# Modulations of the first gated network: from weighted row sums turned by TensorE to one multiply-and-sum per transposed weight tile

## The chip, the core and the metric

The kernel runs on one core of a Trainium2 chip. Its work is shared by TensorE (matrix products, PE in the profile, PEld for its weight loads), VectorE (DVE), ScalarE (ACT), GpSimd (POOL) and SyncE (SP), which here issues nearly all transfers; 16 DMA engines carry them. Each engine has a queue of its own and works it off in order. The metric is the device time of one execution in microseconds, as a median of several runs.

## The reference

A decoder trunk of two layers over 512 tokens of 1024 channels. The first layer mixes tokens with a state-space layer (S5), the second with forgetting attention; behind each stands a gated network with a convolution of width 3. So there are four sub-layers, numbered 0 to 3: S5, first gated network, attention, second gated network. Each is modulated by one conditioning vector `c` of 1024 numbers:

```python
def adaln_params(c, w, b):
    mod = jax.nn.silu(c) @ w + b
    shift, scale, gate = jnp.split(mod, 3, axis=-1)

def modulate(x, g, shift, scale):
    return rmsnorm(x, g) * (1.0 + scale) + shift

hn = modulate(h, norm_g[i, 1], shift, scale)
f = conv_ffn(hn, ffn_w_up[i], ffn_conv_w[i], ffn_conv_b[i], ffn_w_down[i])
h = (h + gate * f).astype(x.dtype)
```

The weights `w` of one modulation are 1024 x 3072 in float32, 12 MB for each sub-layer. The three thirds of its result are the shift (third 0), the scale (third 1) and the gate (third 2). What the change touches is how `silu(c) @ w + b` is computed for some of these thirds.

## The kernel before, in words

Channels lie on the 128 partitions and tokens along the free dimension; 1024 channels are 8 such tiles (`KT`). Large products are made in three parts from a high and a low part of each factor (L301 in the helper `mms`): ScalarE rounds a weight tile to its high part (L284), VectorE subtracts to get the low part (L285), TensorE multiplies three times.

A modulation is wanted in columns: `par[i]` holds for sub-layer i 24 columns of 128 partitions (shift in 0 to 7, scale in 8 to 15, gate in 16 to 23), since channels lie on partitions. `ga[i]` is (1 + scale) times the norm's weight, 8 columns. `sc` is silu(c) as 128 x 8, made by ScalarE at the very start (L102).

There are two ways in which the kernel makes them:

- `ada_pe`, in the S5 stage, for sub-layer 0 and for shift and scale of sub-layer 1: weight tiles go through TensorE against `sc` (L217), and the row that comes out is turned into columns by `ada_columns`.
- `ada_units`, in the first gated network, for the gate of sub-layer 1 and all thirds of sub-layers 2 and 3: seven thirds in five groups ([2] of 1, [0, 1] and [2] of 2, [0, 1] and [2] of 3). For each third, eight tiles of 128 x 1024 (128 of the 1024 inputs, all 1024 outputs of the third) are loaded into two buffers (L240). VectorE multiplies each by the column of `sc` for these inputs and adds it to an accumulator of 128 x 1024 (L243 for the first tile, L245 for the other seven). TensorE then sums the accumulator over partitions by products with ones (L251, four to a third in the profile), ScalarE copies the rows (L255). At the end of a group, `ada_columns` turns the rows into columns on TensorE: the bias comes in by a product with the identity (L160), the rows by products with a selector (L165), and VectorE and ScalarE write `ga` (L170) and `par` (L173).

The work of `ada_units` is cut into steps, one for each weight tile. `build` puts the five groups on the list `bg`, and the gated network takes one step (`tick`) after each of its products: 22 up products, 8 down products, 22 up, and 6 of the last down products (the last two belong to the tail). The 56 tiles fit these 58 ticks. The first of them is taken after the first up product.

The compiler's scheduler sets the order on each engine from when it expects operands to be ready, except in the first part of S5, where `manual_schedule` keeps the order of the program on TensorE, ScalarE, VectorE and SP. In the gated network one rule is written by hand: the first VectorE instruction of each third is put behind the last low part that the norm has made (`issue_after(self.last_lo.ins)`).

The network's head (its first three up products) is worked by halves of the tokens: while TensorE multiplies the first half, the statistics of the second half's norm are taken by TensorE (L385), VectorE makes the inverse root from them (L396 to L406), TensorE spreads it to rows (L415), VectorE multiplies by `ga` (L435), ScalarE makes the high part (L438) and VectorE the low part (L439).

At the start of the kernel SP issues, in this order: the parameters with `c`, x in four pieces of 512 KB, the rest of the constants, then the weights of the modulation of sub-layer 0 for `ada_pe` (L188), S5's first weights and constants.

The attention has a VectorE instruction that adds, takes the minimum along the free dimension and writes both (L1445), followed in the profile by a read of the accumulator.

Of the kernel before, what the change touches and what calls it, by code (L numbers as in the profile page):

```python
# [8 lines left out]
F32 = mybir.dt.float32  # L9
F32R = mybir.dt.float32r  # L10
I32 = mybir.dt.int32
AF = mybir.ActivationFunctionType
ALU = mybir.AluOpType
# [4 lines left out]
P = 128  # L18
D = 1024
KT = D // P  # L20
S = 512
# [22 lines left out]
TAIL_OFF = {"w_hi": 80, "w_lo": 112}, {"w_hi": 96, "w_lo": 0}  # L44

GROUPS = (11, 11)
QGROUPS = (6, 5, 6, 5)
TAIL = 4
FIRST = (("c", (KT,)), ("s5_prm", (3, G // 2)), ("s5_eye", (64,)))
# [12 lines left out]
class Trunk:  # L62
# [138 lines left out]
    def ada_pe(self, i, thirds, late=False):  # L201
# [9 lines left out]
        for step in steps:  # L211
# [15 lines left out]
                self.ada_columns(i, 8 * thirds[0], 8 * thirds[-1] + 8, rows)  # L227
            yield True

    def ada_units(self, i, thirds):  # L230

        nc = self.nc
        thirds = list(thirds)
        rows = self.bgpool.tile([P, S], F32, name="ada_rows", bufs=1)
        n = 0
        for t in thirds:
            acc = self.bgpool.tile([P, D], F32, name="ada_acc", bufs=1)
            for k in range(KT):
                w = self.bgpool.tile([P, D], F32, name="ada_raw", bufs=2)
                nc.sync.dma_start(w, self.io["ada_w"][i, k * P:(k + 1) * P, t * D:(t + 1) * D])  # L240
                if k == 0:
                    with self.tc.issue_after(self.last_lo.ins):
                        nc.vector.tensor_scalar(acc, w, self.sc[:, 0:1], None, op0=ALU.mult)  # L243
                else:
                    nc.vector.scalar_tensor_tensor(  # L245
                        acc, w, self.sc[:, k:k + 1], acc, op0=ALU.mult, op1=ALU.add
                    )
                if k == KT - 1:
                    ps = self.aux.tile([P, S], F32, name="aux")
                    for q in range(2):  # L250
                        nc.tensor.matmul(  # L251
                            ps[32 * q:32 * q + 32, :], self.ones[:, :32], acc[:, q * S:(q + 1) * S],
                            start=True, stop=True, tile_position=(0, 32 * q), skip_group_check=True,
                        )
                    nc.scalar.activation(rows[32 * n:32 * n + 64], ps[:64], AF.Copy)  # L255
                    n += 2
                    if t == thirds[-1]:
                        self.ada_columns(i, 8 * thirds[0], 8 * thirds[-1] + 8, rows[:32 * n])
                yield True


    def finish_norm(self, n=NORM_AFTER):

# [323 lines left out]
    def ffn(self, i, l, x, nxt, ticks=0, plain=None):  # L587

        nc, tc = self.nc, self.tc
        with tc.tile_pool(name=f"ffn{l}", bufs=1, reuse_waits="tile") as pool:  # L590
            self.bgpool = pool
            groups = QGROUPS if plain else GROUPS
            first = [sum(groups[:q]) for q in range(len(groups) + 1)]
            keep, g = {}, {}

            def gate_room(q):
                tag = f"{q % 2}" if plain else ""
                g[q] = [pool.tile([P, groups[q], S], F32R, name=n, tag=n + tag) for n in ("ghi", "glo")]

            if plain:  # L600
                self.gap(pool, 32, "g_gap")
                gate_room(0)
                b = [pool.tile([P, KT // 2, S], F32, name=f"x{j}", tag=n) for j, n in enumerate(("ghi1", "glo1"))]
            conv = self.wide(pool, "conv_wb", {}, F32, 0 if plain else 8, 0, [P, 4, FT])
            nc.sync.dma_start(conv, self.io["conv"][l])
            cw, cb = conv[:, :3], conv[:, 3]

            def gated(m, ps, cols):
                f = m // 2
                if m % 2 == 0:  # L610
                    t = pool.tile([P, S], F32, name="conv", bufs=2 if plain else 3)
                    nc.scalar.activation(t, ps, AF.Identity, bias=cb[:, f:f + 1], scale=cw[:, 2, f:f + 1])
                    for d in (1, 2):
                        nc.vector.scalar_tensor_tensor(  # L614
                            t[:, d:], ps[:, :S - d], cw[:, 2 - d, f:f + 1], t[:, d:], op0=ALU.mult, op1=ALU.add
                        )
                    nc.scalar.activation(t, t, AF.Silu)  # L617
                    keep[f] = t
                    return
                t = keep.pop(f)  # L620
                nc.vector.tensor_tensor(t, t, ps, ALU.mult)
                q = sum(f >= n for n in first[1:])
                j = f - first[q]
                if q not in g:
                    gate_room(q)
                hi, lo = g[q]
                self.put_parts(hi[:, j, :], lo[:, j, :], t)

            after, y = nxt
            def up(fs, **k):  # L630
                self.odd = bool(plain)
                self.product(self.io["w_up"][l], range(2 * fs[0], 2 * fs[-1] + 2), KT, x, gated, ticks=ticks, **k)
                self.odd = False

            last = len(groups) - 1
            down = lambda q, ms, **k: self.product(
                self.io["w_down"][l][:, :, first[q]:first[q + 1], :], ms, groups[q], g[q],
                self.add_residual(i, q == last), after=after, ticks=ticks, **k
            )
            todo = []  # L640
            for q, n in enumerate(groups):
                fs = range(first[q], first[q + 1])
                if not plain:
                    up(fs, head=0 if q else 3)
                    if q < last:
                        down(q, range(KT))
                    continue
                for j, f in enumerate(fs):
                    if f == 0:
                        up([0, 1], head=3, apart=True)  # L650
                        todo.append(self.forms_x(pool, x, b))
                    elif f in plain:
                        if f > 1:
                            up([f], apart=True)
                        for _ in range(4):
                            if todo and next(todo[0], True):
                                todo.pop()
                    else:
                        while todo:
                            if next(todo[0], True):  # L660
                                todo.pop()
                        self.quarters(pool, l, f, x, gated)
                    if q:
                        down(q - 1, range(j * KT // n, (j + 1) * KT // n))
            down(last, range(KT), tail=TAIL if plain else 2, tail_pool=(pool, 4, TAIL_OFF[l]))
        return y
# [121 lines left out]
class S5(Trunk):  # L788
# [291 lines left out]
    def s5(self, i, nxt):  # L1080
        nc, tc = self.nc, self.tc
# [4 lines left out]
        with ExitStack() as stack:  # L1086
# [3 lines left out]
            with ExitStack() as start:  # L1090
                tp = spool("s5t", start)
                self.load_first(tp)
                w = {}
# [9 lines left out]
                with tc.manual_schedule(engines={ENG.PE, ENG.Activation, ENG.DVE, ENG.SP}):  # L1103
                    self.load_x(self.act)
                    self.load_rest()
                    self.s5_planes(keep)
                    ps = self.mm.tile([P, S], F32, name="mmp")
                    for k in range(KT):
# [3 lines left out]
                    rows = self.tmp.tile([P, S], F32, name="nm_t")  # L1112
# [19 lines left out]
                    ps = self.mm.tile([P, S], F32, name="mmp")  # L1132
# [29 lines left out]
            pool = self.s5r = spool("s5r", stack)  # L1162
# [86 lines left out]
            next(ada[1])  # L1249
        self.load_x(self.ctx.enter_context(tc.tile_pool(name="resid", bufs=1, reuse_waits="tile")))  # L1250
        with tc.tile_pool(name="s5b", bufs=1, reuse_waits="tile") as pool:
            self.bgpool = pool
            self.gap(pool, 32, "z_gap")
            zhi = pool.tile([P, KT, S], F32R, name="zhi")
            zlo = pool.tile([P, KT, S], F32R, name="zlo")

            def glu(m, ps, cols):
                t = self.tmp.tile([P, S], F32, name="nm_t")
                nc.scalar.activation(t, ps, AF.Sigmoid)  # L1259
                nc.vector.tensor_tensor(tok(t), tok(t), self.s5_read_y(pool, m), ALU.mult)  # L1260
                self.put_parts(zhi[:, m], zlo[:, m], t)

            for m in range(HEAD):
                glu(m, gps[m], slice(0, S))
            self.product(self.io["s5_w_glu"], range(HEAD, KT), KT, (yhi, ylo), glu)
            after, y = nxt
            self.product(self.io["s5_w_out"], range(KT), KT, (zhi, zlo), self.add_residual(i), tail=2, after=after)
# [245 lines left out]
def lay_out(inp):  # L1513

    f = {n: np.asarray(v) for n, v in inp.items()}
    o = {}
# [8 lines left out]
    o["c"] = cols(f["c"][0], KT)  # L1525
    o["ident"] = np.eye(P, dtype=np.float32)
    o["ada_w"] = f["ada_w"].reshape(4, D, 3 * D)
    o["ada_b"] = cols(f["ada_b"].reshape(4, 3 * D), 24)
    o["norm_g"] = cols(f["norm_g"].reshape(4, D), KT)
    o["final_g"] = cols(f["final_g"], KT)  # L1530
# [22 lines left out]
    w = f["fox_w_in"][0]  # L1553
# [38 lines left out]
```

## Time and profile before

| | |
|---|---|
| median of 3 runs (lowest to highest) | 1244.78 us (1244.68 to 1244.86) |
| the profiled execution's own time | 1247.16 us |
| its span, first to last instruction | 1245.4 us |
| mean granted TensorE clock | 0.993 |
| first gated network, about | 262 to 640 us |
| weight tiles of `ada_units` loaded (first to last issue) | 56 of 512 KB (270.2 to 577.6 us) |
| data moved over the span | 183.24 MB |

How to read it: times are microseconds from the span's start. Engine busy times overlap, so they don't add up to the span. The chain of work that ended last is followed back from the last instruction, at each step to what released it or to the instruction before it on its engine; what doesn't lie on it could be shorter without the end moving at once. A group's row gives line, engine, operation, tile written and tiles read, shapes and count, then busy time and the mean of one in ns, then the idle time ahead of it and what ended that. In a row of the waits stand the engine that waited, what it waited for, the total, the number of times and the longest. A row of the transfers gives the count, the size of one and the median time from issue to landing.

### The profile page before, as it was taken

What the parts mean: (1) busy time and instruction counts of PE and PEld (TensorE: products, weight loads), DVE (VectorE), ACT (ScalarE), POOL (GpSimd) and SP (SyncE); (2) the same over time, 40 slices, a digit from 0 to 9 for tenths busy, and PEclk for the clock granted to TensorE, in tenths of its full rate; (3) what the DMA queues carried; (4) which work ended last, traced back from release to release, by engine and by line L of the source; (5) the groups of instructions that cost most, each with busy time, mean ns of one, the idle gap of its engine ahead of it and who ended that gap; (6) DMA issues with size and microseconds to landing.
All of it is one profiled execution on the core that took longest, in us unless ns stands there. A gap on an engine that the chain in (4) does not pass through costs nothing.

```text
span 1245.4 us, 19609 instructions
## 1 busy us (share of the span) xinstructions
PE 1221.6 (98%) x7584; PEld 1023.6 (82%) x7584; DVE 896.0 (72%) x1610; ACT 564.9 (45%) x1043; POOL 57.1 (5%) x109
## 2 busy tenths in 40 slices
PE   7999999999999999999999999999989999999997
PEld 2566677898778887788799888888989999999987
DVE  7978886569756547566457467665799978888865
ACT  3543455335333223333434366654456555555543
POOL 0000000000000000000000143331000000000000
PEclk9999999999999999999999999999999999999999
DMA  9768667336745646455423344240313332333331
GB/s 353 249 226 261 197 180 255 102 110 193 252 133 176 197 157 219 139 182 165 142 68 102 126 137 134 94 141 15 124 47 113 108 117 89 112 107 106 102 85 69
DMA packets 73068, 183.24 MB, mean 147 GB/s; under 512 B 23079, under 2 KB 25471, under 8 KB 71951
## 3 DMA queue, kind: packets, MB, share of 16 engines
q1 hardware_dynamic: 72687, 181.46, 45.2%
q8 instruction: 60, 0.98, 0.3%
q10 hardware_dynamic: 288, 0.52, 0.1%
q14 instruction: 33, 0.27, 0.1%
HBM read 175.04 MB, written 6.92 MB: 146 GB/s over the span
## 4 chain that ended last, share of the span: by engine, by line
PE 93%; DVE 2%; DMA 2%; issue 1%; ACT 1%; SPq 0%; DVEq 0%; ACTq 0%
PE mmp L301 57%; PE mmp L556 10%; PE mmp L1171 4%; PE aux L556 4%; PE mmp L1337 3%; PE aux L976 2%; PE aux L1480 2%; PE aux L1463 1%; PE mmp L217 1%; PE aux L1057 1%; PE aux L1065 1%; PE aux L1433 1%; PE mmp L1111 1%; PE aux L1015 1%; DMA raw<-in_s_w_glu 1%
## 5 line engine op out<-in xcount | busy, mean ns | idle before, releaser
L284 ACT ACTIVATE w_hi<-raw 128x1024 fp32r<-128x1024 f32 (+4 forms) x197 | 181.4, 927 | 258.6 <-PE mmp L301 211.7
L285 DVE TENSOR_TENSOR w_lo<-raw,w_hi 128x1024 fp32r<-128x1024 f32 (+4 forms) x197 | 210.4, 1070 | 91.9 <-ACT w_hi L284 84.5
L301 PE MATMUL mmp<-a_hi,w_hi 128*128 128x512 f32 (+1 forms) x664 | 243.9, 369 | 2.6 <-ACT nm_t L1259 1.8
L301 PE MATMUL mmp<-a_hi,w_lo 128*128 128x512 f32 (+1 forms) x664 | 240.8, 363 | 3.1 <-DVE w_lo L285 3.1
L301 PE MATMUL mmp<-a_lo,w_hi 128*128 128x512 f32 (+1 forms) x664 | 240.1, 362 | 0.0
L301 PEld LDWEIGHTS mmp<-a_hi,w_hi 128*128 128x128 f32 x664 | 125.8, 190 | 24.7 <-issue 2.6
L301 PE MATMUL mmp<-ghi,w_hi 128*128 128x512 f32 (+1 forms) x394 | 144.8, 367 | 0.0
L301 PEld LDWEIGHTS mmp<-a_hi,w_lo 128*128 128x128 f32 x664 | 125.7, 190 | 22.9 <-DVE w_lo L285 3.3
L301 PE MATMUL mmp<-glo,w_hi 128*128 128x512 f32 (+1 forms) x394 | 144.3, 366 | 0.0
L301 PE MATMUL mmp<-ghi,w_lo 128*128 128x512 f32 (+1 forms) x394 | 144.2, 366 | 0.0
L301 PEld LDWEIGHTS mmp<-a_lo,w_hi 128*128 128x128 f32 x664 | 126.1, 190 | 17.7
L368 DVE SCALAR_TENSOR_TENSOR h<-mmp,par,h 128x512 f32<-128x512 f32 (+1 forms) x74 | 49.8, 676 | 57.0 <-PE mmp L301 56.9
L301 PEld LDWEIGHTS mmp<-ghi,w_lo 128*128 128x128 f32 x394 | 74.0, 188 | 12.1
L301 PEld LDWEIGHTS mmp<-ghi,w_hi 128*128 128x128 f32 x394 | 74.0, 188 | 11.5
L301 PEld LDWEIGHTS mmp<-glo,w_hi 128*128 128x128 f32 x394 | 74.0, 188 | 11.5
L245 DVE SCALAR_TENSOR_TENSOR ada_acc<-ada_raw,sc,ada_acc 128x1024 f32<-128x1024 f32 x49 | 62.8, 1281 | 27.2 <-DMA ada_raw<-in_ada_w 26.9
L556 PE MATMUL mmp<-w_lo,w_hi 128*128 128x256 f32 x216 | 59.7, 276 | 0.0
L556 PE MATMUL mmp<-w_hi,w_lo 128*128 128x256 f32 x216 | 59.7, 276 | 0.0
L556 PE MATMUL mmp<-w_hi 128*128 128x256 f32 x216 | 59.7, 276 | 0.0
L1171 PE MATMUL mmp<-a_x,raw 128*128 128x512 f32 x112 | 56.6, 644 | 0.0
L617 ACT ACTIVATE conv<-conv 128x512 f32<-128x512 f32 x44 | 27.6, 632 | 63.5 <-DVE conv L614 62.7
L285 DVE TENSOR_TENSOR w_lo<-sums,w_hi 128x1024 fp32r<-128x1024 f32 x40 | 48.5, 1221 | 3.6 <-ACT w_hi L284 2.6
(304 smaller groups left out, 2481.2 us busy)
## 6 DMA issues: line engine op xcount, KB each, us to landing
raw<-in_w_up SPq DMA_DIRECT2D x88, 512.0 KB, 3.3
ada_raw<-in_ada_w SPq DMA_DIRECT2D x56, 512.0 KB, 4.3
raw<-in_ada_w SPq DMA_DIRECT2D x40, 512.0 KB, 6.2
raw<-in_w_down SPq DMA_DIRECT2D x32, 384.0 KB, 3.2
raw<-in_w_down SPq DMA_DIRECT2D x32, 320.0 KB, 2.9
nf<-nfd SPq DMA_DIRECT2D x8, 1152.0 KB, 5.7
raw<-in_fox_qk SPq DMA_DIRECT2D x16, 512.0 KB, 3.5
h<-in_x SPq DMA_DIRECT2D x8, 512.0 KB, 5.4
```

What stands on the lines that cost most here:

```text
L217: self.last_mm = nc.tensor.matmul(ps[32 * qq:32 * qq + 32, :], self.sc32[:, k, :], w[:, q * S:(q + 1) * S], start=(step is steps[0]), stop ...
L245: nc.vector.scalar_tensor_tensor(acc, w, self.sc[:, k:k + 1], acc, op0=ALU.mult, op1=ALU.add)
L284: nc.scalar.activation(hi, src, AF.Copy)
L285: nc.vector.tensor_tensor(lo, src, hi.bitcast(F32), ALU.subtract)
L301: self.last_mm = self.nc.tensor.matmul(o, wt, xt[:, cols], start=(k == 0 and n == 0), stop=(k == nk - 1 and n == 2),)
L368: self.nc.vector.scalar_tensor_tensor(self.h[:, m, cols], ps, self.par[i][:, 16 + m:17 + m], self.h[:, m, cols], op0=ALU.mult, op1=ALU.add,)
L556: self.last_mm = nc.tensor.matmul(o, wt[:, k], xt[:, k], start=(first and k == 0 and n == 0), stop=(k == H - 1 and n == 2), skip_group_che ...
L617: nc.scalar.activation(t, t, AF.Silu)
L976: nc.tensor.matmul(ps[g2][:, j, cols], x[rows, a + j, r].rearrange("p c j -> p (c j)"), self.rr[rows, planes, q, :], start=(j == 0 and r = ...
L1171: nc.tensor.matmul(ps, w[m][:, k, :], x[:, k], start=(k == 0), stop=(k == KT - 1))
L1337: self.last_mm = nc.tensor.matmul(ps[q, b][:, :n], xt[:, k, tb], wt, start=(k == 0 and i == 0), stop=(k == KT - 1 and i == 2),)
L1480: nc.tensor.matmul(pv[:, c * P:], self.v[:, hp, k, r].rearrange("p t d -> p (t d)"), pp[:, r, c + 3 * k:NB + 3 * k, :].rearrange("p b t -> ...
```

## The change

In `ada_units` a tile now holds 128 of the outputs on its partitions and all 1024 inputs along the free dimension: the weights of sub-layers 1 to 3 are laid out once more on the host, transposed (`ada_rows`, 24 tiles of 128 x 1024 for each sub-layer, every tile contiguous). For each tile VectorE makes one multiply-and-sum (`tensor_tensor_reduce`): the tile times silu(c) along the free dimension, which lies spread to all partitions in `crow`, summed with the bias as the first value, and written as one column of `par[i]`. The products are written over the tile. When column 15 is made, VectorE makes `ga[i]` from columns 8 to 15.

With it go the accumulator, the sums over partitions, the rows and the turning in this network, and the hand-written order rule. `ada_columns` and `ada_pe` stay for the S5 stage. Two transfers are new: `spread_c` writes `sc` to a row of 1024 numbers in DRAM, in SP's queue of the first part of S5, behind the constants and ahead of the weights, in pieces of one number each, as the row runs across the 8 columns and 128 partitions; `ada_pool` reads that row back to all 128 partitions (512 KB) when the first gated network begins. Loads, ticks and the number of tiles stay as they are, as do the groups and their order.

```diff
+ROWS_FROM = 1
...
+    def spread_c(self):
+
+        self.cd = self.dram.tile([1, D], F32, name="c_row")
+        self.nc.sync.dma_start(self.cd.rearrange("o (k p) -> p (o k)", p=P), self.sc)
+
+    def ada_pool(self, pool, bufs):
+
+        self.bgpool, self.ada_bufs = pool, bufs
+        self.crow = pool.tile([P, D], F32, name="ada_c")
+        self.nc.sync.dma_start(self.crow, self.cd.to_broadcast([P, D]))
+
     def ada_units(self, i, thirds):
 
         nc = self.nc
-        thirds = list(thirds)
-        rows = self.bgpool.tile([P, S], F32, name="ada_rows", bufs=1)
-        n = 0
         for t in thirds:
-            acc = self.bgpool.tile([P, D], F32, name="ada_acc", bufs=1)
-            for k in range(KT):
-                w = self.bgpool.tile([P, D], F32, name="ada_raw", bufs=2)
-                nc.sync.dma_start(w, self.io["ada_w"][i, k * P:(k + 1) * P, t * D:(t + 1) * D])
-                if k == 0:
-                    with self.tc.issue_after(self.last_lo.ins):
-                        nc.vector.tensor_scalar(acc, w, self.sc[:, 0:1], None, op0=ALU.mult)
-                else:
+            for m in range(8 * t, 8 * t + 8):
+                w = self.bgpool.tile([P, D], F32, name="ada_raw", bufs=self.ada_bufs)
+                nc.sync.dma_start(w, self.io["ada_rows"][i - ROWS_FROM, m])
+                nc.vector.tensor_tensor_reduce(
+                    w, w, self.crow, 1.0, self.ada_b[:, i, m:m + 1], ALU.mult, ALU.add, self.par[i][:, m:m + 1]
+                )
+                if m == 15:
                     nc.vector.scalar_tensor_tensor(
-                        acc, w, self.sc[:, k:k + 1], acc, op0=ALU.mult, op1=ALU.add
+                        self.ga[i], self.par[i][:, 8:16], 1.0, self.norm_g[:, i, :], op0=ALU.add, op1=ALU.mult
                     )
-                if k == KT - 1:
-                    ps = self.aux.tile([P, S], F32, name="aux")
-                    for q in range(2):
-                        nc.tensor.matmul(
-                            ps[32 * q:32 * q + 32, :], self.ones[:, :32], acc[:, q * S:(q + 1) * S],
-                            start=True, stop=True, tile_position=(0, 32 * q), skip_group_check=True,
-                        )
-                    nc.scalar.activation(rows[32 * n:32 * n + 64], ps[:64], AF.Copy)
-                    n += 2
-                    if t == thirds[-1]:
-                        self.ada_columns(i, 8 * thirds[0], 8 * thirds[-1] + 8, rows[:32 * n])
                 yield True
...
         with tc.tile_pool(name=f"ffn{l}", bufs=1, reuse_waits="tile") as pool:
-            self.bgpool = pool
+            if not plain:
+                self.ada_pool(pool, 2)
...
                     self.load_x(self.act)
                     self.load_rest()
+                    self.spread_c()
                     self.s5_planes(keep)
...
     o["ada_w"] = f["ada_w"].reshape(4, D, 3 * D)
+    o["ada_rows"] = np.moveaxis(o["ada_w"][1:], 1, 2).reshape(3, 24, P, D)
```

More of the change, by code (lines that the diff above doesn't have):

```diff
@@ L1251, in s5 @@
         with tc.tile_pool(name="s5b", bufs=1, reuse_waits="tile") as pool:
-            self.bgpool = pool
             self.gap(pool, 32, "z_gap")
```

## The prediction

> **What bounds the kernel now.** I read the page first, then the chain of work that ended last over the stretch of the changed network, then the stage table for what the other engines have spare there.
>
> ```profile
> PE 1221.6 (98%) x7584; PEld 1023.6 (82%) x7584; DVE 896.0 (72%) x1610; ACT 564.9 (45%) x1043; POOL 57.1 (5%) x109
> ...
> PE 93%; DVE 2%; DMA 2%; issue 1%; ACT 1%; SPq 0%; DVEq 0%; ACTq 0%
> ```
>
> TensorE (PE) is busy in 98% of the span and carries 93% of the chain that ended last. In such a kernel a microsecond taken off TensorE's queue is a microsecond off the time, unless something else turns out late. The first gated network runs from about 262 to 640 us; the stage table, in two stretches of it (busy time of each engine, the granted clock, the DMA share):
>
> ```profile
> core 0: us, PE busy (x) PEld busy (x) DVE busy (x) ACT busy (x) POOL busy (x), PEclk, DMA share, GB/s
> 270.00:282.00 12.00, 11.24 (x93) 10.93 (x93) 10.21 (x31) 4.86 (x11) 0.00 (x0) 1.00 0.56 179
> 282.00:640.00 358.00, 358.00 (x1658) 292.73 (x1656) 220.60 (x254) 123.63 (x167) 0.12 (x1) 1.00 0.55 175
> ```
>
> From 282 us on TensorE has no gap: 358.00 of 358.00. VectorE (DVE) has 358.00 − 220.60 = 137.4 us free, ScalarE more, the DMA engines 45%. The only holes are in the first 12 us. So I look at what TensorE does there for the modulations. The chain shows it piece by piece (start, duration, what); this is the first third of the network, and the one row in which a later group differs:
>
> ```profile
> 316.59 0.98 PE aux L251 x4
> 317.57 0.32 PE aux L160 x2
> 317.89 1.25 PE mmp L301 x5
> 319.14 0.98 PE aux L165 x8
> 320.12 42.62 PE mmp L301 x187
> ...
> 413.65 0.79 PE aux L165 x8
> ```
>
> All of these lie on the chain, between products of L301, with nothing beside them on TensorE.
>
> **What the change removes.** The counts in the network, from the groups by line:
>
> ```profile
> L251 PE MATMUL aux<-ada_acc,ones 128*32 128x512 f32 x28 | 7.4, 605 | 0.0
> L165 PE MATMUL aux<-sel,ada_rows 64*128 64x2 f32 (+1 forms) x40 | 5.0, 247 | 0.0
> L160 PE MATMUL aux<-rest 128*128 128x8 f32 (+1 forms) x10 | 2.0, 269 | 0.0
> ```
>
> L251 (sums over partitions) comes 28/4 = 7 times, once a third: 7 × 0.98 = 6.86 us. L160 comes 10/2 = 5 times, once a group of thirds: 5 × 0.32 = 1.60. L165 comes 40/8 = 5 times; a group of one third costs 0.98, one of two thirds 0.79: 3 × 0.98 + 2 × 0.79 = 4.52. Together 12.98 us. The products squeezed between run slower than usual: 5 in 1.25 us where 187 in 42.62 us make 5 × 0.228 = 1.14. That is about 0.11 a group, 0.5 for five. **Gain on TensorE: 13.5 us.** ScalarE's copies of rows and columns go as well; ScalarE isn't on this path, so they count as nothing.
>
> **What VectorE gets instead.** 56 multiply-and-sums of 128x1024 take the place of 49 + 7 older instructions. The old forms, the nearest form of the new one (the attention's fused add-and-min, which has the same accumulator output), and a slow outlier:
>
> ```profile
> L245 DVE SCALAR_TENSOR_TENSOR ada_acc<-ada_raw,sc,ada_acc 128x1024 f32<-128x1024 f32 x49 | 62.8, 1281 | 27.2 <-DMA ada_raw<-in_ada_w 26.9
> L243 DVE TENSOR_SCALAR ada_acc<-ada_raw,sc 128x1024 f32<-128x1024 f32 x7 | 5.2, 748 | 0.0
> L1445 DVE CUSTOM_DVE_ANT_0 s<-mmp,nf 128x512 f32<-128x512 f32 x14 | 9.0, 677 | 0.0
> L1445 DVE CUSTOM_DVE_ANT_0 s<-aux,nf 128x384 f32<-128x384 f32 x16 | 8.1, 546 | 0.0
> L1445 DVE DVE_READ_ACCUMULATOR2_ANT mn<- 128x1 f32 x64 | 5.3, 83 | 0.0
> L1260 DVE TENSOR_TENSOR nm_t<-nm_t,yt 128x512 f32<-128x512 f32 x8 | 9.1, 1167 | 1.3 <-DMA yt<-s_yd 0.9 <-ACT nm_t L1259 0.5
> ```
>
> From 384 to 512 elements the fused form grows by 131 ns, so to 1024 it adds 4 × 131: 677 + 524 = 1.20 us, plus 0.08 for reading the accumulator: 1.28 us a tile, 56 × 1.28 = 71.9 us against 62.8 + 5.2 = 68.0. The lower end is the form at its fastest with the read hidden, 1.20; the upper end the outlier's rate doubled for 1024, 2.33 + 0.08 = 2.41 us. I take 1.28, since form and rate are the same. The 4 us more lie in 137 us of free VectorE time: cost nothing. At the upper end it is 56 × 1.13 = 63 us more, still inside the 137.
>
> The two small products for scale (at column 15) replace L170 one for one. Tiles per tick, loads (56 of 512 KB) and buffers (2) are unchanged, so each modulation is finished at the same tick, long before its reader. A load still waits for the second-last tile's reader, and what stands behind it in SP's queue are the weights of the products:
>
> ```profile
> SPq L240 <- DVE ada_acc L245: 65.8, 47, 3.4
> ...
> DVE ada_acc L245 <- DMA ada_raw<-in_ada_w: 26.9, 17, 3.5
> ```
>
> SP already stands 65.8 us at these loads and VectorE 26.9 us for their data, and TensorE lost nothing by it. With equal durations I count no change; if that cover went, weights would be late by at most the longest such wait, 3.5 us, at a time.
>
> **The start.** The new write of the conditioning vector, 1024 pieces of 4 bytes, goes into SP's queue behind x and ahead of the first modulation weights. The DMA engines are full there, by a row of the stage table:
>
> ```profile
> 28.00:32.00 4.00, 4.00 (x15) 1.08 (x14) 4.00 (x8) 0.00 (x0) 0.00 (x0) 1.00 1.04 412
> ```
>
> The transfers to compare with, by the median time from issue to landing:
>
> ```profile
> u<-s_ud SPq DMA_DIRECT2D x8, 256.0 KB, 4.6
> s_yd<-yg SPq DMA_DIRECT2D x8, 256.0 KB, 2.9
> ...
> nfd<-nf_rows SPq DMA_DIRECT2D x1, 16.0 KB, 1.5
> ```
>
> And the timeline of that stage (start, duration), with the landing time of its last modulation weights, from the DMA view of the moment of their issue:
>
> ```profile
> 2.78 0.21 ACT L102 ACTIVATE sc<-first 128x8 f32<-128x8 f32 x1 [0.77 <-DMA first<-in_first]
> ...
> 3.85 15.70 SPq L188 DMA_DIRECT2D raw<-in_ada_w  x10
> ...
> 20.07 5.95 SPq L188 DMA_DIRECT2D raw<-in_ada_w  x6
> ...
> 34.95 1.06 PE L217 MATMUL mmp<-raw,sc 128*32 128x512 f32 x8
> ```
>
> ```profile
> raw<-in_ada_w SPq DMA_DIRECT2D x1, 512.0 KB, 8.4
> ```
>
> The last of the six loads is issued one issue (some 0.3 us) ahead of 20.07 + 5.95, at about 25.7, and lands 8.4 us later, at 34.1; its product starts at 34.95. So 0.85 us of delay is free, the rest goes to the chain. No row shows 4-byte pieces. The write s_yd, also 1024 pieces (of 256 bytes), takes 2.9 us, of which 1.5 is what a small transfer takes anyway: it holds the queues for 1.4 us. The read u, 4.6 − 1.5 = 3.1. Lower end: nothing held. I take 1.4, the write of as many pieces: cost 1.4 − 0.85 = **0.5 us**, between 0 and 2.25. SP's wait for the vector itself is no cost: SP reaches that place at 3.85 us, and ScalarE has made it by 2.99.
>
> Against this stands a rule of the Trainium skill. "DMA: Bandwidth & Descriptors", section Specifications, asks for 512 bytes or more and says that below this the DMA engine does a read-modify-write; its Rules for kernel authors say that a non-contiguous last dimension becomes one descriptor per element, and to avoid it. The 256-byte write of this trace is under that limit too and shows only the 1.4 us; what 4 bytes do no run here shows. If the rule doubled that hold, the start would cost 2.8 − 0.85 = 1.95 us in place of 0.5, and the sum would be −11.25.
>
> **The head of the network.** The old code kept the first instruction of each third behind the norm (the wait on its last low part); the new one has no such rule, so the scheduler may put the first multiply-and-sums into VectorE's queue earlier, among the norm's second half. The chain there, and VectorE's timeline:
>
> ```profile
> 278.85 0.46 PE aux L415 x4
> ...
> 279.33 0.49 DVE nm_h L435
> ...
> 279.85 0.52 ACT a_hi L438
> ```
>
> ```profile
> 279.33 1.27 DVE L435 SCALAR_TENSOR_TENSOR nm_h<-h,ga,aux 128x256 f32<-128x256 f32 x3 [0.99 <-PE aux L415]
> ...
> 285.92 0.75 DVE L243 TENSOR_SCALAR ada_acc<-ada_raw,sc 128x1024 f32<-128x1024 f32 x1
> ```
>
> VectorE, ScalarE and TensorE stand in one chain here, and VectorE has a gap of 0.99 us. A tile of 1.28 us put into it makes the chain later by 0.3; a second one (two buffers allow no third) by 1.28 more, 1.6 in all; none at all costs 0. I take one: **0.3 us**. The broadcast of the vector is one more load of 512 KB in a stretch with a DMA share of 0.56, and lands as the first weights do: nothing.
>
> **Sum.** −13.5 + 0.5 + 0.3 = −12.7 us. The profiled execution took 1247.16 us with a span of 1245.4; the median shown is 1244.78. All terms lie in the span, so I take them off the median: **1232.1 us**.
>
> **Rivals.**
> - *A wait takes the place of the order rule.* Both first tiles are queued ahead of the norm's second half before their data have landed: 1.6 plus the longest wait for such a load, 3.5, instead of 0.3: 1244.78 − 13.5 + 0.5 + 5.1 = 1236.9. For it: nothing holds them now. Against: the loads are issued from 270.15 and land in some 4.3 us, four before the gap. Chance 0.10.
>
> ```profile
> 270.15 1.46 SPq L240 DMA_DIRECT2D ada_raw<-in_ada_w  x2
> ...
> ada_raw<-in_ada_w SPq DMA_DIRECT2D x56, 512.0 KB, 4.3
> ```
>
> - *The scattered write fills the queues.* At the mean packet of the busy queue, 45.2% of 16 engines' span over 72687 packets or 0.124 us, 64 pieces an engine hold 7.9 us, 7.1 past the slack: 1244.78 − 13.5 + 7.1 + 0.3 = 1238.7. The skill's rule above would make it so. Against: s_yd. Chance 0.08.
>
> ```profile
> q1 hardware_dynamic: 72687, 181.46, 45.2%
> ```
>
> - *Weights come late once TensorE is quicker*, and half of the gain is given back: 1244.78 − 6.8 + 0.8 = 1238.8. Against: TensorE is only 13.5/358 = 3.8% quicker in the stage, and all others have more spare. Chance 0.05.
> - *VectorE becomes the bound, slower than before.* Without the modulations VectorE has 220.6 − 68.0 = 152.6 us of work in the stage. With 56 tiles it fills the shorter stage of 358 − 13.5 = 344.5 us at 191.9/56 = 3.43 us a tile, and the time passes that of before at (358 − 152.6)/56 = 3.67. At 4.0 us a tile the stage takes 152.6 + 224 = 376.6, 18.6 more than before: 1263.4. Against: that is far above even the outlier's 2.41. Chance 0.04.
> - *The code doesn't do what it says* (TensorE's sums stay, hidden elsewhere): within 0.2% of before. The diff takes them out; chance 0.02.
>
> The forecast keeps 0.71. Its own bounds: start 0 to 2.25, head 0 to 1.6, so 1231.3 to 1235.1; the two waits of TensorE for weights in the network (1.7 us below) may go too, so 1229.6 below.
>
> ```profile
> PEld mmp L301 <- ACT w_hi L284: 1.7, 2, 0.8
> ```
>
> Forecast and first rival hold 0.81, so the range is 1229.6 to 1237.0. A measurement of this kernel tells about 0.2%, 2.5 us, from no change. Faster than that: 0.71 + 0.10 + 0.08 + 0.05 = 0.94, less 0.01 for the tail of the late weights, 0.93; within it 0.02 and that 0.01, 0.03; slower 0.04.
>
> **What would show it.** Right: no L251, and L160 and L165 only in the S5 stage, TensorE still without gaps from 282 us on, the stage 13 us shorter; one multiply-and-sum near 1.2 us and a read near 0.08; the product that starts at 34.95 later by half a microsecond; nm_h at the head later by 0.3. Wrong: DMA waits of TensorE before 36 us (second rival), a tile ahead of nm_h that waits for a load (first), TensorE waiting for w_hi or w_lo in the network (third), VectorE full there (fourth).

## The result and the profile after

The changed kernel takes 1240.35 us in the median against 1244.88 us before, a ratio of 0.9965 with a 95% interval of 0.9955 to 0.9975: faster, by about a third of the 12.7 us that were forecast, and 3.35 us above the upper end of the range. The profiled execution of the changed kernel took 1243.44 us. One of the ten executions of experiment 5 took 2037.20 us at a granted clock of 0.554, against 0.989 to 0.994 in the other nine, and is left out of its median and ratio.

The sums and turns of TensorE are gone from the network, as the diff says. The rest of the gain went to two places. On the page of the changed kernel, the shares of the chain that ended last:

```profile
PE 83%; DMA 7%; DVE 5%; issue 2%; ACT 1%; POOL 0%; SPq 0%; DVEq 0%; POOLq 0%; ACTq 0%
PE mmp L297 47%; PE mmp L552 10%; DMA ada_raw<-in_ada_rows 5%; PE mmp L1169 5%; PE aux L552 4%; PE mmp L1334 3%; PE aux L973 2%; PE mmp L1198 2%; PE aux L1477 2%; PE mmp L218 1%; PE aux L1460 1%; DVE ada_raw L249 1%; PE aux L1062 1%; PE aux L1054 1%; DVE w_lo L281 1%
```

TensorE carried 93% of the chain before and carries 83% now; of the 10 points, 5 went to DMA (7%, from 2%) and 3 to VectorE (5%, from 2%). A transfer that nobody should wait for, the weight tiles of the modulations, stands in it with 5%.

To see where, I cut the span at three marks that every version has: the first statistics of the first network's norm (products into `aux`), the first high part of that norm's second half, and the statistics behind the network. From the chain of the kernel before (the middle mark stands in the prediction):

```profile
262.20 0.34 PE aux L385 x4
...
639.74 0.34 PE aux L385 x4
```

and from the chain of the changed kernel:

```profile
267.02 0.34 PE aux L381 x4
...
285.88 0.52 ACT a_hi L434
...
634.98 0.34 PE aux L381 x4
```

| stretch | before | after | difference |
|---|---|---|---|
| to the first statistics (S5 stage) | 262.20 | 267.02 | +4.82 |
| head of the network, to the second half's high part | 17.65 | 18.86 | +1.21 |
| the network, to its last statistics | 359.89 | 349.10 | −10.79 |
| what follows | 605.66 | 606.42 | +0.76 |
| span | 1245.4 | 1241.4 | −4.0 |

**The start.** The chain of the changed kernel over its first 32 us (start, duration, what):

```profile
3.71 13.94 DMA c_row<-sc
...
17.66 10.54 DMA raw<-in_ada_w
...
31.43 0.18 DVE ga L171
```

From VectorE's timeline of the kernel before:

```profile
26.22 0.16 DVE L170 SCALAR_TENSOR_TENSOR ga<-aux,rest 128x8 f32<-128x8 f32 x1
```

The write of 4 KB takes 13.94 us to land, and the first `ga`, at 26.22 before, comes at 31.43: 5.2 us later. The stage table of the changed kernel for the same time says what the queues did (the last two columns are the DMA share and GB/s):

```profile
8.00:12.00 4.00, 4.00 (x9) 1.28 (x8) 3.79 (x32) 2.51 (x5) 0.00 (x0) 1.00 1.43 211
12.00:16.00 4.00, 3.28 (x10) 1.01 (x8) 2.26 (x19) 1.69 (x3) 0.00 (x0) 1.00 0.87 56
...
48.00:52.00 4.00, 4.00 (x6) 1.59 (x5) 3.86 (x9) 4.00 (x7) 0.00 (x0) 0.50 0.80 256
```

The kernel before, in the same two stretches:

```profile
8.00:12.00 4.00, 4.00 (x6) 1.41 (x5) 3.79 (x32) 1.78 (x3) 0.00 (x0) 1.00 1.04 408
12.00:16.00 4.00, 4.00 (x10) 1.27 (x8) 2.28 (x19) 1.99 (x4) 0.00 (x0) 1.00 1.03 408
```

The DMA engines are busy and move little: 211 and then 56 GB/s where 408 went before. The two stretches lack 4 us × (197 + 352) GB/s = 2.2 MB, or 5.4 us of full queues. SP stands still as well. By its own waits up to 45 us, it held back loads of weights until two earlier transfers had landed, the constants (issued ahead of the write) and the write itself; the kernel before waits 0.2 us for the constants and has no such write:

```profile
SPq L189 <- DMA rest<-in_rest: 4.0, 1, 4.0
SPq L189 <- DMA c_row<-sc: 3.5, 1, 3.5
```

A third row of the stage table shows something that came on top, the granted clock at 0.50 from 48 to 52 us (1.00 there before).

**The network.** The timeline of VectorE in the head of the changed kernel (start, duration, engine, line, operation):

```profile
281.68 1.28 DVE L249 CUSTOM_DVE_ANT_0 ada_raw<-ada_raw,ada_c,rest 128x1024 f32<-128x1024 f32 x1
282.88 0.08 DVE L249 DVE_READ_ACCUMULATOR2_ANT par<- 128x1 f32 x1
282.88 0.17 DVE L401 TENSOR_SCALAR rs_t<-rs_t 128x2 f32<-128x2 f32 x1
282.96 1.28 DVE L249 CUSTOM_DVE_ANT_0 ada_raw<-ada_raw,ada_c,rest 128x1024 f32<-128x1024 f32 x1
...
285.37 1.26 DVE L431 SCALAR_TENSOR_TENSOR nm_h<-h,ga,aux 128x256 f32<-128x256 f32 x3
```

Both first tiles stand ahead of `nm_h`, inside the inverse root of the second half. One tile takes 1.28 us from start to start, as forecast. And by the view of the tile `ada_raw`, all loads are issued by 447 us, where before they lasted to 577.6:

```profile
L248 SPq DMA_DIRECT2D ada_raw<-in_ada_rows x56: 327/328/437, 276.2 to 447.4; - x56
```

The tiles no longer keep to their products; they run as fast as the loads allow, and VectorE, which works its queue in order, stands at them for data. In the kernel before, VectorE was through with the second third at 340.87 us and began the next one only at 365.38, after TensorE had summed the accumulator (362.74 to 363.72). Two lines of VectorE's timeline and one of the chain:

```profile
339.60 1.27 DVE L245 SCALAR_TENSOR_TENSOR ada_acc<-ada_raw,sc,ada_acc 128x1024 f32<-128x1024 f32 x1
...
365.38 0.75 DVE L243 TENSOR_SCALAR ada_acc<-ada_raw,sc 128x1024 f32<-128x1024 f32 x1
```

```profile
362.74 0.98 PE aux L251 x4
```

The chain of the changed kernel during the first down products, which read the gated products in a high and a low part (`ghi`, `glo`):

```profile
398.48 4.62 DMA ada_raw<-in_ada_rows
...
403.24 1.29 DVE ada_raw L249
...
404.53 0.59 DVE conv L611
405.12 0.86 DVE ada_raw L249
...
406.39 0.60 DVE conv L618
406.99 0.73 DVE w_lo L281
407.73 0.66 DVE glo L281
```

The last gated products of the first group come late, since tiles with their loads stand between the steps that make them, and TensorE stops inside the first down product. From the waits of TensorE over the network:

```profile
PE mmp L297 <- ACT ghi L280: 2.1, 1, 2.1
```

and the stage row around it, with TensorE busy for 17.79 of 20 us and a clock of 0.91:

```profile
400.00:420.00 20.00, 17.79 (x71) 13.95 (x70) 14.42 (x24) 4.95 (x7) 0.00 (x0) 0.91 0.77 247
```

### The profile page after: what moved, and what is told of

The parts are those of the page before. It is cut to its first block, busy times and chain, and to the rows that moved or that the text cites. A ratio compares the mean times of both kernels' runs of the same rounds, so it can differ in the third digit from the quotient of the medians.

```text
span 1241.4 us, 19480 instructions
## 1 busy us (share of the span) xinstructions
PE 1213.7 (98%) x7506; PEld 1018.6 (82%) x7506; DVE 899.3 (72%) x1666; ACT 560.5 (45%) x1031; POOL 56.5 (5%) x109
## 4 chain that ended last, share of the span: by engine, by line
PE 83%; DMA 7%; DVE 5%; issue 2%; ACT 1%; POOL 0%; SPq 0%; DVEq 0%; POOLq 0%; ACTq 0%
PE mmp L297 47%; PE mmp L552 10%; DMA ada_raw<-in_ada_rows 5%; PE mmp L1169 5%; PE aux L552 4%; PE mmp L1334 3%; PE aux L973 2%; PE mmp L1198 2%; PE aux L1477 2%; PE mmp L218 1%; PE aux L1460 1%; DVE ada_raw L249 1%; PE aux L1062 1%; PE aux L1054 1%; DVE w_lo L281 1%
## 5 line engine op out<-in xcount | busy, mean ns | idle before, releaser
L249 DVE CUSTOM_DVE_ANT_0 ada_raw<-ada_raw,ada_c,rest 128x1024 f32<-128x1024 f32 x56 | 71.7, 1282 | 29.0 <-DMA ada_raw<-in_ada_rows 28.9
```

Source lines behind the costliest of these rows:

```text
L249: nc.vector.tensor_tensor_reduce(w, w, self.crow, 1.0, self.ada_b[:, i, m:m + 1], ALU.mult, ALU.add, self.par[i][:, m:m + 1])
```

## The experiments

The theory: (A) the write of the vector blocks the full queues at the start, and its 1024 pieces are why; (B) without the order rule and without the accumulator the scheduler runs the tiles ahead of their products, which costs once in the head and once in the first down products. The rivals: the late start is the half-speed clock by chance, not the write; TensorE's stop comes from VectorE's load or from the transfers as such; and for (A) in itself, number, size, place or neighbourhood of the pieces. Line numbers in a view are those of that run's own kernel, so the same line of the program can stand a few numbers further on.

| run | median | before, same runs | ratio (95%) |
|---|---|---|---|
| before + write | 1252.89 | 1245.48 | 1.0055 (1.0036 to 1.0075) |
| changed, wide pieces | 1234.27 | 1245.48 | 0.9915 (0.9895 to 0.9935) |
| changed, paced | 1238.78 | 1245.48 | 0.9940 (0.9923 to 0.9958) |
| changed, paced, wide pieces | 1229.62 | 1245.48 | 0.9871 (0.9851 to 0.9891) |
| changed, head rule alone | 1241.61 | 1245.48 | 0.9970 (0.9956 to 0.9984) |
| before + 1024 pieces of 32 bytes | 1246.10 | 1245.48 | 1.0004 (0.9994 to 1.0015) |
| before + 1024 pieces of 4 bytes, apart | 1246.31 | 1245.48 | 1.0008 (0.9995 to 1.0020) |
| paced, late write | 1237.55 | 1245.48 | 0.9936 (0.9918 to 0.9953) |
| paced, no write | 1230.26 | 1245.39 | 0.9886 (0.9865 to 0.9906) |
| paced, wide pieces, again | 1231.45 | 1245.39 | 0.9887 (0.9860 to 0.9915) |

**1. The write alone, in the kernel before.**

```diff
                     self.load_rest()
+                    self.spread_c()
                     self.s5_planes(keep)
```

> The kernel before, with the scattered write of the vector alone added at its place in the start (nothing reads it). If the write is what makes the start late: it lands some 14 us after its issue (after: 13.9), VectorE's first ga comes at about 31.4 us in place of 26.2, and the time is 5 to 9 us above the kernel before, about 1250 to 1254. If the late start of the changed kernel is only the half-speed clock that fell there by chance: ga stays within 1 us of 26.2, the time within 2.5 us of before.

It costs 0.55%, 7 us. From its DMA view and the view of the tile `ga`:

```profile
c_row<-sc SPq DMA_DIRECT2D x1, 4.0 KB, 14.4
```

```profile
L170 DVE SCALAR_TENSOR_TENSOR ga<-aux,rest x4: 166/167/167, 31.9 to 571.8; 128x8 f32<-128x8 f32 x4
```

Landing 14.4 us after the issue, first `ga` at 31.9. The head (17.66 us) and the network (359.88) are those of before. So the write makes the late start, with nothing else of the change present, and its 7 us are about half of what the network gains.

**2. The same vector in 128 pieces of 32 bytes.** The row keeps the order in which a partition holds its eight numbers; the weight tiles' inputs are laid out in the same order.

```diff
-        self.nc.sync.dma_start(self.cd.rearrange("o (k p) -> p (o k)", p=P), self.sc)
+        self.nc.sync.dma_start(self.cd.rearrange("o (p k) -> p (o k)", p=P), self.sc)
```

> The changed kernel, the vector written in 128 pieces of 32 bytes in place of 1024 of 4 bytes (the weight tiles' inputs stand in the same new order). If the cost goes with the number of pieces: about an eighth of it is left, the write lands some 7 us after its issue (the queue ahead of it) and ga comes at about 26.5 to 27 us; the time is 5 to 6 us below the changed kernel, about 1234.5 to 1235.5. If the cost is the place in the queue or the wait for the vector: as the changed kernel, about 1240.

```profile
c_row<-sc SPq DMA_DIRECT2D x1, 4.0 KB, 6.3
```

The first `ga` comes at 25.0 us, before that of the kernel without any write (26.2), and the ratio falls from 0.9965 to 0.9915, about what the write alone added. The start costs nothing in this form. The cost is gone, more fully than the expectation by the number of pieces had it; but this run changes the pieces' size and number together, so it can't say which of them counts. The head (18.87) and the stop of TensorE for `ghi` (3.6 us here) stay, as they should.

**3. Each tile behind its own product.** `evacuated` is the last VectorE instruction of the product's evaluation.

```diff
-                nc.vector.tensor_tensor_reduce(
+                with self.tc.issue_after(self.evacuated.ins):
+                    nc.vector.tensor_tensor_reduce(
...
-            self.nc.vector.scalar_tensor_tensor(
+            self.evacuated = self.nc.vector.scalar_tensor_tensor(
```

> The changed kernel, each multiply-and-sum put behind the last VectorE instruction of the product of its own step, so that none runs ahead. If running ahead is what costs in the network: the head is 1.2 us shorter (two tiles no longer ahead of the second half of the norm), the stop of TensorE before the first down products (2.1 us in the changed kernel, and a half-speed clock window after it) is gone, TensorE has no gap from the end of the head to 640 us, and the time is 3 to 4 us below the changed kernel, about 1236.5 to 1237.5. If it is VectorE's load or the loads themselves: still a stop of 1 to 2 us, time within 1 us of the changed kernel.

The marks of the paced kernel, from its chain:

```profile
267.92 0.34 PE aux L382 x4
...
285.58 0.52 ACT a_hi L435
...
630.38 0.34 PE aux L382 x4
```

The head is back at 285.58 − 267.92 = 17.66 us, and the network takes 344.80: 4.30 less than in the changed kernel and 15.09 less than before. TensorE's only waits in the network are the 0.8 us for `a_hi` and 0.2 in the head that it had before. The same 56 loads and 56 multiply-and-sums are there, only later (the tiles run from 298.7 to 610.5 us), so neither VectorE's load nor the transfers as such made the stop. Nor is it the sum of VectorE's waits for the tiles' data: that is 26.9 us before, 28.9 in the changed kernel and 1.1 here, and before it cost TensorE nothing; what changed is where those waits stand. The time is 0.25% below that of the changed kernel; the stretches say 0.44%, with 0.9 us given back in the S5 stage and 0.8 behind the network in the profiled run. The two intervals leave room for both. The median, 1238.78, stands above the 1236.5 to 1237.5 expected.

**4. Both edits.**

> Both edits together, pieces of 32 bytes and each tile behind its own product. If the two costs are separate and are all that stands between forecast and result: the gain of TensorE less under 1 us, 12 to 13.5 us below the kernel before, about 1231.5 to 1233. If something else in the change costs as well: above 1235.

1229.62 us, a ratio of 0.9871: 16 us below before, more than the 12 to 13.5 expected. The network is again 344.80 us long and the S5 stage has no late start (`ga` at 25.3). By the ratios the two edits gain 0.50 and 0.25 points alone and 0.94 together, each within about 0.2, so the runs agree with two separate costs and show no third one between the forecast and the result.

**5. The old order rule alone.**

```diff
+                with self.tc.issue_after(self.last_lo.ins):
+                    nc.vector.tensor_tensor_reduce(
```

> The changed kernel with the old order rule alone put back: every multiply-and-sum stands behind the norm's last low part, as the first of each third did before, and nothing holds it to its own product. If only the head suffers from running ahead: the head (first statistics to first high part of the second half) takes 17.65 us again in place of 18.86, and the rest of the network (349.10 us in the changed kernel) comes down to the 344.8 of the paced one. If running ahead costs at both places by itself: the head is cured and TensorE still stops 2 to 4 us ahead of the first down products, the rest of the network takes 348 to 351 us; the time is 1 to 1.5 us below the changed kernel.

```profile
270.23 0.34 PE aux L382 x4
...
287.88 0.52 ACT a_hi L435
...
635.46 0.34 PE aux L382 x4
```

Head 17.65 us: cured. Network 347.58: between the two expectations' numbers, 2.8 us above the paced kernel, and TensorE still stops for `ghi` (1.3 us). So the hand-written rule guarded the head alone. What is left to have kept the other tiles to their products is the accumulator, whose next third had to wait for TensorE's sum of the last, as the kernel before shows at 340.87 to 365.38 us; no run put this dependence alone back. The time expected, 1 to 1.5 us below the changed kernel, wasn't measured: the two ratios lie within each other's interval.

**6 and 7. Number, size or neighbourhood of the pieces.** Both in the kernel before, writing to a row that nobody reads.

```diff
+        cd = self.dram.tile([KT, P, 8], F32, name="c_row")
+        self.nc.sync.dma_start(cd.rearrange("k p e -> p k e"), self.ones[:, :64].rearrange("p (k e) -> p k e", e=8))
```

> The kernel before, with a write of 1024 pieces of 32 bytes (eight times the bytes, from a tile of ones, read by nothing) at the same place. If the number of pieces sets the cost: as with 1024 pieces of 4 bytes, landing some 14 us after the issue, first ga at 31 to 32 us, 6 to 8 us above the kernel before. If it is that sixteen pieces fall on the same 64 bytes of memory: most of the cost is gone, ga at 26.5 to 28 us.

```diff
+        cd = self.dram.tile([KT, P, 16], F32, name="c_row")
+        self.nc.sync.dma_start(cd[:, :, 0].rearrange("k p -> p k"), self.sc)
```

> The kernel before, with the write of 1024 pieces of 4 bytes, each piece 64 bytes from the next (read by nothing). If the number of pieces sets the cost, or their size below a limit: landing some 14 us after the issue, first ga at 31 to 32 us, 6 to 8 us above the kernel before. If pieces that fall on the same 64 bytes are what is slow: landing 6 to 8 us after the issue, ga at 26.5 to 28 us.

Both carry as many packets as the write of experiment 1 (1040 more than the kernel before in the queue of SP's transfers). From the DMA views of the first and the second:

```profile
c_row<-ones SPq DMA_DIRECT2D x1, 32.0 KB, 6.8
```

```profile
c_row<-sc SPq DMA_DIRECT2D x1, 4.0 KB, 7.7
```

And the stage table of the second, with 4-byte pieces apart, where the changed kernel has 211 and 56 GB/s:

```profile
8.00:12.00 4.00, 4.00 (x6) 1.50 (x5) 3.79 (x32) 1.27 (x3) 0.00 (x0) 1.00 1.09 326
12.00:16.00 4.00, 4.00 (x9) 1.36 (x9) 2.18 (x18) 2.51 (x4) 0.00 (x0) 1.00 1.02 414
```

The first `ga` comes at 25.1 and 26.7 us, and neither time differs from before. Number and size alone are thereby both out: 1024 pieces of 4 bytes, 64 bytes apart, cost nothing that can be measured, and the same number of the same pieces side by side costs 7 us. What is slow is small pieces packed side by side, sixteen to 64 bytes (from sixteen partitions) and all 1024 in 4 KB. Two pieces to 64 bytes, as in the run with 32 bytes, are not slow. The spread pieces also lie over 64 KB in place of 4, so these runs don't tell whether sharing 64 bytes or crowding into a wider stretch is what hinders, nor whether the order in which the pieces come plays a part.

**8. The place.**

```diff
+        with self.tc.issue_after(self.x_load.ins):
+            self.spread_c()
```

> The paced kernel, the write in 1024 pieces of 4 bytes moved out of the start to the end of the S5 stage, behind the second load of x, where the queues are a third full. If the place makes the cost (full queues and weights that TensorE waits for): the start is as before (ga at 26 us) and the time is that of the paced kernel with wide pieces, 1229 to 1231. If the write costs wherever it stands: 1234 or more, with weights late somewhere behind it.

This missed the place it aimed at: the scheduler issues the second load of x early, and the write went out with it at 182.79 us, ahead of the gated output of S5. The start is clean (`ga` at 26.0), but the time is 1237.55. The chain of this kernel and its stage table show why:

```profile
182.41 13.02 DMA yt<-s_yd
```

```profile
184.00:188.00 4.00, 4.00 (x19) 3.34 (x18) 0.00 (x0) 0.00 (x0) 0.00 (x0) 1.00 1.59 266
188.00:192.00 4.00, 3.18 (x15) 2.29 (x13) 0.00 (x0) 0.00 (x0) 0.00 (x0) 1.00 0.71 27
192.00:196.00 4.00, 0.00 (x0) 0.00 (x0) 0.00 (x0) 0.55 (x1) 0.00 (x0) 0.98 0.80 117
```

Again some 8 us in which the queues are busy and move little (27, then 117 GB/s), and here it holds up even a read that was issued 0.4 us ahead of it (13.02 us, against 3.3 for a usual one). TensorE is idle from 192 to 196 us. So the start isn't special: the write costs at this second place too, where TensorE waits for a transfer issued beside it. A place where nothing waits is left open.

**9 and 10. No write, and the best version again.** c lies in memory as a row of its own; ScalarE takes the silu on all partitions.

```diff
+        self.nc.sync.dma_start(self.crow, self.io["c_row"].to_broadcast([P, D]))
+        with self.tc.issue_after(self.last_hi.ins):
+            self.nc.scalar.activation(self.crow, self.crow, AF.Silu)
```

> The paced kernel with no write at all: c lies in memory as a row, is read to all partitions when the network begins, and ScalarE takes its silu there, behind the norm's last high part. If the write in 32-byte pieces still costs something at the start: ga comes up to 0.5 us earlier than with it (25.3 us) and the time is up to 1 us below the paced kernel with wide pieces. If that write is free: the same time within 1 us, or a little more from the 1 us of ScalarE in the network's head.

> The paced kernel with wide pieces once more, beside the one without a write on the same chip: 1229 to 1231.5, the network 344.8 us long from its first high part of the second half to its last statistics, as in the paced kernel.

0.9886 and 0.9887, with the first `ga` at 26.1 us without a write and at 24.9 with it, and the network 344.80 and 344.79 us long: the write in wide pieces is free, so far as this can tell. Either version is the best found, some 14 us below the kernel before and 9 to 10 below the changed one.

## Why the prediction was wrong, step by step

**What bounds the kernel** was read rightly: TensorE's queue. Where the other costs are taken away, all of TensorE's part arrives.

**TensorE's gain of 13.5 us** was right in kind and too small: 15.09 in the paced kernel. The missing 1.6 us lie at L251. The chain gives each set a piece of 0.98 us, but the distance from one up product to the next but one tells more. From ScalarE's timeline, with one such set between, before:

```profile
358.08 0.76 ACT L612 ACTIVATE conv<-mmp,conv_wb 128x512 f32<-128x512 f32 x1
...
370.17 0.76 ACT L612 ACTIVATE conv<-mmp,conv_wb 128x512 f32<-128x512 f32 x1
```

and in the paced kernel:

```profile
350.30 0.76 ACT L610 ACTIVATE conv<-mmp,conv_wb 128x512 f32<-128x512 f32 x1
361.18 0.76 ACT L610 ACTIVATE conv<-mmp,conv_wb 128x512 f32<-128x512 f32 x1
```

12.09 against 10.88: 1.21 us for a set, 0.23 more than its piece. Taken for all seven sets, 7 × 0.23 = 1.6; only this one is shown here. The changed kernel kept 10.79 of it, because of the next point but two.

**VectorE's tile** at 1.28 us was right as a number, and by luck in its parts: it was forecast as 1.20 for the form and 0.08 for the read of the accumulator behind it. The form alone takes 1282 ns in the mean of 56, and the read (83 ns) lies inside it, at 282.88 in a tile that runs from 281.68 to 282.96.

**The start, 0.5 us,** is the step that failed most. "The write of as many pieces" was taken as 1.4 us from s_yd, whose 1024 pieces are of 256 bytes and lie in memory of their own; the row didn't show what makes this write slow. The free 0.85 us was read at the last six loads of weights, and no run shows whether it was right, for the delay came in earlier: at the first eight loads, whose products make `ga`. The second rival had the mechanism and nearly the price (7.9 us of queues held; 5.4 us lacking in two stretches, `ga` 5.2 us late, 7 us of time), with a chance of 0.08. That the price came so near is luck, since its reason was not the right one: the mean packet doesn't explain it, as the same number of packets without such neighbours costs nothing here. The Trainium skill ("DMA: Bandwidth & Descriptors", Specifications) gives 512 bytes as the least size for full rate and says that below it a read-modify-write is done. All pieces tried here are below it, the slow and the free, so in these runs that limit alone doesn't tell them apart. The range should have reached to 1239: the prediction itself said that no row shows 4-byte pieces, yet bounded them by rows of 256 bytes.

**The loads and the tiles' order, counted as no change,** is the second step that failed. It held that tiles per tick, loads and buffers stay the same, so each modulation comes at the same tick. But a tick only sets the order of the program; what held the work back to it was, by the trace of the kernel before and by what experiment 5 leaves over, the accumulator's wait for TensorE, which the change took away. It cost 4.3 us in the network (344.80 paced, 349.10 changed). Of these, 2.2 are TensorE's idle time in the row from 400 to 420 us, and by an estimate from the clock of 0.91 in the same row (0.09 × 20 us) 1.8 are slower products; whether the stop calls the slower clock was not settled.

**The head, 0.3 us,** was right in place and mechanism and too small: both first tiles went ahead of `nm_h`, 1.21 us. The first rival named two tiles with a wait for loads; the tiles came, at 281.68 and 282.96, without such a wait.

Put together by the stretches: −15.09 + 4.30 + 1.21 + 4.82 + 0.76 = −4.0 us, the difference of the two spans. In the 4.82 of the S5 stage lie the 5.2 us of the write, the granted clock at half speed from 48 to 52 us, and what was won back later: the kernel before shows a clock of 0.94 from 70 to 100 us and 0.97 from 200 to 262, the changed one 1.00 in both; the write alone made that stage 7.88 us longer in its own kernel (270.08 against 262.20). How the clock's share came about, and whether the waiting of TensorE called it, was not settled: the wide-piece kernel has no wait of TensorE for a load above 0.23 us there, and its product behind the start also took 8.81 us in place of 7.15.

## What to carry to other kernels

When a dependence is removed, ask what else it did: an accumulator that waits for another engine also paces the work behind it, and without it a scheduler runs independent work ahead into queues that are worked in order. For the new small transfer here the bytes said nothing, and a row with as many pieces said little; look at where the pieces land, and at what stands in the same queues, for this transfer held up all that followed without having a reader. Here a layout that keeps each partition's eight numbers together did away with the cost.

## What the runs showed of the hardware

A write of 1024 pieces of 4 bytes, sixteen neighbours to 64 bytes, lands after 12.8 to 14.5 us. At the start of the kernel 5.4 us of full queues go missing beside it, and the kernel with this write alone takes 7 us longer; in another place a read issued 0.4 us ahead of it took 13.02 us in place of 3.3. Spread 64 bytes apart it lands after 7.7 us in the same place of the queue and costs nothing that can be measured (1.0008, 0.9995 to 1.0020). And the piece that the chain gives to a small product between large ones (0.98 us) was less than what taking it out gained (1.21 us).
